# The latents' weights turned and split in six pieces over the query products, turned blocks tied behind the newest low part

## The chip, the cores and the metric

One core of one Trainium2 chip runs the whole program. The metric is device time in microseconds (us), the median of several executions. The engines in the text are TensorE (PE, matmuls), VectorE (DVE), ScalarE (ACT), GpSimd (POOL) and SyncE (SP, which here only issues DMAs).

## The reference, cut to what matters

The program is one decoder layer at 256 positions and width 2048, in float32: a mixer of two attention branches, a cross-attention over 256 memory tokens, and a SwiGLU feed-forward part, each followed by a layer norm.

```python
proj = x @ w_in                                    # 2048 -> 9552 columns
q_dsa, c_kv, q_idx, k_idx, w_idx, q_m, k_m, v_m, ga, gb = jnp.split(proj, points, axis=-1)
...
q_lat = jnp.einsum('shd,hdc->shc', q, w_uk)        # w_uk: 8 heads x 128 x 256 latents
...
o = jnp.einsum('shc,hcd->shd', o_lat, w_uv)        # w_uv: 8 heads x 256 x 128
...
merged = g_a * (o_a @ w_o_dsa) + g_b * (o_b @ w_o_moba)
return merged @ w_out                              # 2048 x 2048
...
k, v = jnp.split(mem @ w_kv, 2, axis=-1)           # the memory tokens' keys and values
```

## The kernel before, in words

**Products.** Every product streams its weight matrix from HBM once, in chunks of 512 KB (`chunk_in`, `wide`). A chunk lands in a tile `raw` (5 buffers). It is then split into a high and a low part in a tile `hl` (4 buffers): ACT writes the high part (line 116) and DVE writes the low part, the rest (line 117, a two-operand instruction over 128x1024 values). `chunk_mm` (lines 221 to 223) then issues three matmuls for each pair of operands: high by high, high by low, low by high. That makes 12 matmuls of 512 columns for a chunk, two row halves times two blocks of the contraction. The stationary operand is the turned input, held in four "quads" (tiles `b8`, printed as `b`), each with a high and a low half, too.

**Turned blocks.** An input is needed with its contraction along the partitions. `turned` (lines 172 to 184) does it without PE: four DMAs load a block in a permuted order into a tile `turn` (2 buffers), four DVE transposes (line 181) write a tile `tr`, ACT writes the high half (line 182) and DVE the low half (line 184). The generator pauses at each `yield`. Three blocks of `x` are turned so in the first 35 us (`load_x`), four blocks of the memory tokens in the output projection `w_out` (`load_mem`, lines 785 to 795), and the results of many products on the way to the next one.

**The latents' weights.** `latent_weights` (lines 292 to 317) loads `w_uk` and `w_uv` (1 MB each) and works in four pieces: two with four transposes (line 309) and a split, two with a split alone. It is a generator in the queue `side`, which `product` steps once for each chunk. It waits four steps, so all four pieces fall in the eight chunks of the product for the compressed keys, whose end also holds the norm of those keys (lines 386 to 419): small instructions that go back and forth between DVE, ACT, POOL and PE. The pieces are read by `latent_heads`, the next generator in `side`.

**What sets the order.** Each engine executes its instructions in one fixed order. That order is no copy of the code's: a scheduler lays the instructions out by its own simulated times when the program is built, and it may put an instruction ahead of others that the code names first. `tc.issue_after(ins)` forbids that for a block: what is traced in it stands behind `ins` on its engine. Before, it is used only for two loads (lines 693 and 788). All DMAs in this text are issued from SP, also in one order.

Of the kernel before, what the change touches and what calls it, by code (L numbers as in the profile page):

```python
# [1 line left out]

# [1 line left out]

# [8 lines left out]
AF = mybir.ActivationFunctionType  # L13
ALU = mybir.AluOpType
# [3 lines left out]
S = 256  # L18
# [47 lines left out]
def trunk(ctx: ExitStack, tc: tile.TileContext, a, out: bass.AP):  # L66
    nc = tc.nc
# [6 lines left out]
    dram = ctx.enter_context(tc.tile_pool(name="dram", bufs=6, space=bass.MemoryType.DRAM))  # L74
    side = Side()
    last = [None]
    later = []

    def flush():
# [7 lines left out]
    def nm(s):  # L87
        count[0] += 1
        return f"{s}_{count[0]}"
# [13 lines left out]
    def f(ap):  # L103
        return ap.bitcast(F32)
# [9 lines left out]

    def split(hi, lo, src, eng=None):
        nc.scalar.activation(hi, src, AF.Copy)  # L116
        (eng or nc.vector).tensor_tensor(lo, src, f(hi), op=ALU.subtract)  # L117


    ident = const.tile([P, P], F32, name="ident")  # L120
# [6 lines left out]
    for tt in range(NT):  # L127
        k = P * (tt + 1)
# [43 lines left out]
    def turned(hi, lo, src, mixed):  # L172
        n = src.shape[0]
        t = work.tile([P, S // 32, P], F32, tag="turn", name=nm("turn"), bufs=NTURN)[:, :n // 32]
        for i in range(4):
            nc.sync.dma_start(t[32 * i:32 * i + 32], src[:, i * P:(i + 1) * P].rearrange("(t i) c -> i t c", i=32))  # L176
        yield
        tr = work.tile([P, 4, S], F32, tag="tr", name=nm("tr"))[:, :, :n]
        v = t.rearrange("p t (j k) -> p k t j", k=4) if mixed else t.rearrange("p t (k j) -> p k t j", k=4)
        for i in range(4):  # L180
            nc.vector.transpose(tr[:, i, :], v[:, i])  # L181
        nc.scalar.activation(hi, tr, AF.Copy)  # L182
        yield
        nc.vector.tensor_tensor(lo, tr, f(hi), op=ALU.subtract)  # L184
# [8 lines left out]
    def chunk_in(pieces, c, n, held=False, mixed=False, fine=None, eng=None):  # L193
        raw = stream.tile([P, KC, W], F32, tag="raw", name=nm("raw"), bufs=5)
        at = 0
        for w in pieces:
            m = w.shape[1]
            if mixed:
                g = c * KC // 4
                rows = w[g * W:(g + 1) * W, :].rearrange("(p k) n -> p k n", k=4)[:, c * KC % 4:c * KC % 4 + KC, :]  # L200
            else:
                rows = w[c * KC * P:(c + 1) * KC * P, :].rearrange("(k p) n -> p k n", p=P)
            for k in ([slice(i, i + 1) for i in range(KC)] if fine else [slice(0, KC)]):
                last[0] = nc.sync.dma_start(raw[:, k, at:at + m], rows[:, k, :])
                if fine:
                    next(fine, None)
            at += m
        t = b8() if held else stream.tile([P, D], F32R, tag="hl", name=nm("hl"), bufs=4)
        hi, lo = [t[:, i * KC * W:(i + 1) * KC * W].rearrange("p (k n) -> p k n", k=KC) for i in range(2)]
        for k in ([slice(i, i + 1) for i in range(KC)] if fine else [slice(0, KC)]):  # L210
            split(hi[:, k, :n], lo[:, k, :n], raw[:, k, :n], eng)
        return hi, lo

    def chunk_mm(o, act, tt, c, kts, n, w):
# [77 lines left out]
    def latent_weights():  # L292
        raw = b8(F32)
        rows = a["w_uk"][0].rearrange("h d c -> (h d) c")
        for i in range(4):
            nc.sync.dma_start(raw[32 * i:32 * i + 32].rearrange("p (t c) -> p t c", c=LAT // 4),
                              rows[:, i * LAT // 4:(i + 1) * LAT // 4].rearrange("(t i) c -> i t c", i=32))
        rawv = b8(F32)
        for cc in range(2):
            nc.sync.dma_start(rawv[:, cc * 1024:(cc + 1) * 1024].rearrange("p (h d) -> p h d", h=NH),  # L300
                              a["w_uv"][0].rearrange("h (c k) d -> k c h d", k=2)[cc])
        for _ in range(4):
            yield
        for cc in range(2):
            q = b8()
            tr = work.tile([P, 4, S], F32, tag="tr", name=nm("tr")).rearrange("p k t -> p (k t)")
            v = raw.rearrange("p (t j k) -> p k t j", k=2, j=32)[:, cc]
            for g in range(4):
                nc.vector.transpose(tr[:, g * S:(g + 1) * S], v[:, g * 8:(g + 1) * 8])
            split(q[:, :1024], q[:, 1024:], tr)  # L310
            ukT.append(q)
            yield
        for cc in range(2):
            q = b8()
            split(q[:, :1024], q[:, 1024:], rawv[:, cc * 1024:(cc + 1) * 1024])
            uv.append(q)
            yield

# [2 lines left out]
    def wide(wsrc, load, tail=2):  # L321
# [10 lines left out]
        for c in range(ND):  # L332
            raw = stream.tile([P, 2 * W], F32, tag="raw", name=nm("raw"), bufs=5)
            t = stream.tile([P, D], F32R, tag="hl", name=nm("hl"), bufs=4)
            hi, lo = t[:, :2 * W], t[:, 2 * W:]
# [7 lines left out]
                last[0] = nc.sync.dma_start(raw[:, cs], rows)  # L343
                load(c, i)
            for cs in parts:
                split(hi[:, cs], lo[:, cs], raw[:, cs])
            if c < ND - tail:
                for g in range(2):
                    mm(g, c, hi, lo)
# [306 lines left out]
    for j in range(4):  # L656
        cs = slice(j * W, (j + 1) * W)
# [5 lines left out]
    for j in range(4):  # L663
        cs = slice(j * W, (j + 1) * W)
# [3 lines left out]
        for tt in range(NT):  # L668
            g = stage()
# [6 lines left out]
        q = Quad()  # L676
        d = spill()
        for tt in range(NT):
            g = gb[tt]
# [120 lines left out]
    for j in range(4):  # L800
        cs = slice(j * W, (j + 1) * W)
# [55 lines left out]
    for j in range(DFF // W):  # L857
# [13 lines left out]
        q = Quad()  # L871
# [40 lines left out]
```

## Time and profile before

| | us |
|---|---|
| median of 3 runs | 1505.7 (1501.36 to 1506.67) |
| the profiled execution, its own time | 1505.91 |
| its span, first to last instruction | 1504.1 |
| PE busy | 1464.7 (97%) |
| DVE busy | 929.5 (62%) |
| ACT busy | 685.3 (46%) |

The span is what the profile sees. The time of the same execution is 1.8 us longer. Matmuls overlap in the pipeline, so PE's busy time is not a measure of how well PE is used; the number of matmuls in a stretch is.

### The profile page before, as it was taken

Reading aid. Unit: us, or ns where it says so; the run is one execution under the profiler, and the core shown is the slowest. Engines: PE = TensorE matmul, PEld = TensorE weight load, DVE = VectorE, ACT = ScalarE, POOL = GpSimd, SP = SyncE. Lnnn points to the kernel's source line nnn. Section 1 sums busy time; section 2 is a strip of 40 time slices with the busy share of each in tenths; the row PEclk is TensorE's granted clock in tenths of the full one; section 3 lists DMA queues with packets and bytes.
Section 4 is the critical chain, followed back from the end, with each engine's and each line's share of the span. In section 5 each row is a group of like instructions: output and inputs, shape, how many; then the busy total and the mean of one; then the engine's idle time right before and its main releaser. Section 6 shows DMA issues by size and latency. Waiting matters only on the chain.

```text
span 1504.1 us, 17772 instructions
## 1 busy us (share of the span) xinstructions
PE 1464.7 (97%) x6640; PEld 1216.3 (81%) x6640; DVE 929.5 (62%) x1145; ACT 685.3 (46%) x798; POOL 54.1 (4%) x63
## 2 busy tenths in 40 slices
PE   8999999999999999889989999999999999999996
PEld 6978888888888888677878888888888888888885
DVE  6565986575756665777784555555455455545455
ACT  4545456454544443354753444444344444333342
POOL 0000000000000000040020000000000000000003
PEclk9999999999999999999999999999999999999998
DMA  9875667777667789749536666666767667666662
GB/s 281 199 222 161 191 215 224 231 238 226 220 189 226 224 258 280 197 151 319 196 111 208 209 210 220 220 221 210 223 210 214 222 220 251 192 198 193 192 223 82
DMA packets 199703, 318.71 MB, mean 212 GB/s; under 512 B 18880, under 2 KB 60992, under 8 KB 199616
## 3 DMA queue, kind: packets, MB, share of 16 engines
q1 hardware_dynamic: 199616, 317.57, 68.4%
q8 instruction: 52, 0.85, 0.2%
q14 instruction: 35, 0.29, 0.1%
HBM read 299.70 MB, written 17.83 MB: 211 GB/s over the span
## 4 chain that ended last, share of the span: by engine, by line
PE 50%; DVE 3%; DMA 2%; issue 1%; ACT 0%; SPq 0%; POOL 0%; ACTq 0%; DVEq 0%
PE acc L222 16%; PE acc L223 16%; PE acc L221 16%; DVE b L735 1%; DMA spill<-b 1%; DVE b L778 1%; DMA spill<-stage 0%; DMA turn<-spill 0%; ACT b L116 0%; PE aux L156 0%; DVE b L117 0%; DVE hl L117 0%; DVE b L737 0%; SPq L176 0%; DVE b L780 0%
## 5 line engine op out<-in xcount | busy, mean ns | idle before, releaser
L117 DVE TENSOR_TENSOR hl<-raw,hl 128x1024 fp32r<-128x1024 f32 (+2 forms) x493 | 595.9, 1217 | 415.0 <-ACT hl L116 414.2
L116 ACT ACTIVATE hl<-raw 128x1024 fp32r<-128x1024 f32 (+2 forms) x495 | 516.6, 1051 | 582.9 <-PE acc L223 523.5
L222 PE MATMUL acc<-hl,b 128*128 128x512 f32 (+1 forms) x1912 | 746.9, 391 | 13.5 <-DVE hl L117 13.5
L221 PE MATMUL acc<-hl,b 128*128 128x512 f32 (+1 forms) x1912 | 745.1, 391 | 0.7 <-ACT b L116 0.7
L223 PE MATMUL acc<-hl,b 128*128 128x512 f32 (+1 forms) x1912 | 745.1, 390 | 0.0
L222 PEld LDWEIGHTS acc<-hl,b 128*128 128x128 f32 x1912 | 361.4, 189 | 88.9 <-DVE hl L117 16.4
L221 PEld LDWEIGHTS acc<-hl,b 128*128 128x128 f32 x1912 | 361.2, 189 | 74.3 <-ACT b L116 0.9
L223 PEld LDWEIGHTS acc<-hl,b 128*128 128x128 f32 x1912 | 361.3, 189 | 73.9
L181 DVE STREAM_TRANSPOSE tr<-turn 128x256 f32<-128x256 f32 (+1 forms) x156 | 71.2, 515 | 106.7 <-DMA turn<-spill 87.7
L182 ACT ACTIVATE b<-tr 128x1024 fp32r<-128x1024 f32 (+1 forms) x39 | 39.5, 1016 | 123.1 <-DVE tr L181 119.7
L184 DVE TENSOR_TENSOR b<-tr,b 128x1024 fp32r<-128x1024 f32 (+1 forms) x39 | 45.3, 1167 | 3.6 <-ACT b L182 3.0
L116 ACT ACTIVATE b<-aux 128x512 fp32r<-128x512 f32 (+1 forms) x44 | 23.2, 537 | 30.0 <-PE aux L262 16.5
L117 DVE TENSOR_TENSOR b<-aux,b 128x512 fp32r<-128x512 f32 (+1 forms) x44 | 25.9, 609 | 8.6 <-ACT b L116 8.3
L117 POOL TENSOR_TENSOR hl<-raw,hl 128x1024 fp32r<-128x1024 f32 x2 | 4.9, 2456 | 718.9 <-ACT hl L116 718.9
L222 PE MATMUL acc<-b,b 128*128 128x512 f32 x72 | 28.0, 391 | 0.3 <-DVE b L117 0.3
L221 PE MATMUL acc<-b,b 128*128 128x512 f32 x72 | 27.9, 393 | 0.1
L223 PE MATMUL acc<-b,b 128*128 128x512 f32 x72 | 27.9, 390 | 0.0
L117 DVE TENSOR_TENSOR b<-raw,b 128x1024 fp32r<-128x1024 f32 x16 | 23.4, 1484 | 6.7 <-ACT b L116 6.5
L261 PE MATMUL acc<-hl,b 128*128 128x512 f32 x64 | 26.0, 406 | 1.5 <-DVE hl L117 1.5
L262 PE MATMUL acc<-hl,b 128*128 128x512 f32 x64 | 25.6, 404 | 0.0
L261 PE MATMUL aux<-b,b 128*128 128x256 f32 (+1 forms) x80 | 21.9, 282 | 0.0
L262 PE MATMUL aux<-b,b 128*128 128x256 f32 (+1 forms) x80 | 21.0, 279 | 0.0
(135 smaller groups left out, 629.5 us busy)
## 6 DMA issues: line engine op xcount, KB each, us to landing
raw<-in_w_ffn_in SPq DMA_DIRECT2D x176, 512.0 KB, 4.6
raw<-in_w_in SPq DMA_DIRECT2D x143, 512.0 KB, 4.3
raw<-in_w_ffn_out SPq DMA_DIRECT2D x88, 512.0 KB, 4.4
raw<-in_w_out SPq DMA_DIRECT2D x32, 512.0 KB, 5.7
spill<-stage SPq DMA_DIRECT2D x56, 256.0 KB, 4.1
turn<-spill SPq DMA_DIRECT2D x112, 128.0 KB, 3.4
raw<-in_w_o_dsa SPq DMA_DIRECT2D x16, 512.0 KB, 4.5
raw<-in_w_o_moba SPq DMA_DIRECT2D x16, 512.0 KB, 4.8
```

The costliest lines, as they stand in the source:

```text
L116: nc.scalar.activation(hi, src, AF.Copy)
L117: (eng or nc.vector).tensor_tensor(lo, src, f(hi), op=ALU.subtract)
L181: nc.vector.transpose(tr[:, i, :], v[:, i])
L182: nc.scalar.activation(hi, tr, AF.Copy)
L184: nc.vector.tensor_tensor(lo, tr, f(hi), op=ALU.subtract)
L221: nc.tensor.matmul(o[:, :n], xh, hi[:, kk, :n], start=k == 0, stop=False)
L222: nc.tensor.matmul(o[:, :n], xh, lo[:, kk, :n], start=False, stop=False)
L223: nc.tensor.matmul(o[:, :n], xl, hi[:, kk, :n], start=False, stop=k == kts - 1)
L261: nc.tensor.matmul(o, lh, rl, start=False, stop=False)
L262: nc.tensor.matmul(o, ll, rh, start=False, stop=stop)
L735: nc.vector.tensor_tensor(t, t, self.rows[0][:, cs], op=ALU.mult)
L778: nc.vector.tensor_tensor(t, t, self.rows[0][:, cs], op=ALU.mult)
```

## The change: places in the order, and when the latents' weights are split

Three edits. A list `lows` records the DVE instruction of each chunk's low part as it is traced. `behind()` puts a block behind the newest one. The transposes in `turned`, those of `latent_weights`, and the DVE parts of the latter's splits are put in such blocks. And `latent_weights` waits eight steps in place of four, and pauses once more between the high and the low part of each `w_uk` piece, so it makes six pieces, in the query product that follows. No instruction is added or removed.

```diff
+    lows = []
...
     def split(hi, lo, src, eng=None):
         nc.scalar.activation(hi, src, AF.Copy)
-        (eng or nc.vector).tensor_tensor(lo, src, f(hi), op=ALU.subtract)
+        return (eng or nc.vector).tensor_tensor(lo, src, f(hi), op=ALU.subtract)
+
+    def behind():
+
+        return tc.issue_after(lows[-1].ins) if lows else nullcontext()
...
-        for i in range(4):
-            nc.vector.transpose(tr[:, i, :], v[:, i])
+        with behind():
+            for i in range(4):
+                nc.vector.transpose(tr[:, i, :], v[:, i])
         nc.scalar.activation(hi, tr, AF.Copy)
...
-            split(hi[:, k, :n], lo[:, k, :n], raw[:, k, :n], eng)
+            ins = split(hi[:, k, :n], lo[:, k, :n], raw[:, k, :n], eng)
+            if eng is None:
+                lows.append(ins)
...
-        for _ in range(4):
+        for _ in range(8):
             yield
         for cc in range(2):
             q = b8()
...
-            for g in range(4):
-                nc.vector.transpose(tr[:, g * S:(g + 1) * S], v[:, g * 8:(g + 1) * 8])
-            split(q[:, :1024], q[:, 1024:], tr)
+            with behind():
+                for g in range(4):
+                    nc.vector.transpose(tr[:, g * S:(g + 1) * S], v[:, g * 8:(g + 1) * 8])
+            nc.scalar.activation(q[:, :1024], tr, AF.Copy)
+            yield
+            with behind():
+                nc.vector.tensor_tensor(q[:, 1024:], tr, f(q[:, :1024]), op=ALU.subtract)
             ukT.append(q)
             yield
         for cc in range(2):
             q = b8()
-            split(q[:, :1024], q[:, 1024:], rawv[:, cc * 1024:(cc + 1) * 1024])
+            with behind():
+                split(q[:, :1024], q[:, 1024:], rawv[:, cc * 1024:(cc + 1) * 1024])
             uv.append(q)
             yield
...
             for cs in parts:
-                split(hi[:, cs], lo[:, cs], raw[:, cs])
+                lows.append(split(hi[:, cs], lo[:, cs], raw[:, cs]))
```

Where the order of an engine changes at all, it does so in three stretches: the first 35 us, the stretch around the latents' weights, and the output projection. Elsewhere the same instructions stand in the same order.

**Output projection, DVE.** `hl` rows are low parts of chunks of `w_out`, in the order of the chunks; `tr<-turn` rows are the transposes of the memory tokens' first two blocks; `b_730` and `b_739` rows are those blocks' low halves. Before:

```order
L117 TENSOR_TENSOR hl_4838<-raw_4836,hl_4838 128x1024
L181 STREAM_TRANSPOSE tr_4934<-turn_4912 128x256 x4
L117 TENSOR_TENSOR hl_4855<-raw_4853,hl_4855 128x1024
L184 TENSOR_TENSOR b_730_4911<-tr_4934,b_730_4911 128x1024
L117 TENSOR_TENSOR hl_4873<-raw_4871,hl_4873 128x1024
L117 TENSOR_TENSOR hl_4896<-raw_4894,hl_4896 128x1024
L181 STREAM_TRANSPOSE tr_4998<-turn_4976 128x256 x4
L117 TENSOR_TENSOR hl_4919<-raw_4917,hl_4919 128x1024
```

The same engine and place in the changed kernel:

```order
L118 TENSOR_TENSOR hl_4838<-raw_4836,hl_4838 128x1024
L118 TENSOR_TENSOR hl_4855<-raw_4853,hl_4855 128x1024
L118 TENSOR_TENSOR hl_4873<-raw_4871,hl_4873 128x1024
L118 TENSOR_TENSOR hl_4896<-raw_4894,hl_4896 128x1024
L118 TENSOR_TENSOR hl_4919<-raw_4917,hl_4919 128x1024
L187 STREAM_TRANSPOSE tr_4934<-turn_4912 128x256 x4
L118 TENSOR_TENSOR hl_4942<-raw_4940,hl_4942 128x1024
L732 SCALAR_TENSOR_TENSOR b_689_4608<-b_689_4608,acc_4744 128x512
L190 TENSOR_TENSOR b_730_4911<-tr_4934,b_730_4911 128x1024
```

The first four transposes moved behind four more low parts. Those of the second, third and fourth block moved behind four more low parts each in the same way (the second's from ahead of `hl_4919` to behind `hl_4983`). SP's order is the same there.

**Latents' weights, DVE.** `hl_787` and `hl_756` are the second chunk of the first query product in either order, `hl_819` and `hl_774` the third; `tr<-b` are transposes of `w_uk`, `b<-tr` the low parts of its pieces, `b<-b` those of `w_uv`; `stage`, `st`, `mv` and `kn` rows belong to the norm. Before:

```order
L117 TENSOR_TENSOR hl_787<-raw_785,hl_787 128x1024
L309 STREAM_TRANSPOSE tr_607<-b_70_526 128x256 x4
L309 STREAM_TRANSPOSE tr_633<-b_70_526 128x256 x4
...
L117 TENSOR_TENSOR b_84_632<-tr_633,b_84_632 128x1024
L117 TENSOR_TENSOR b_88_658<-b_71_531,b_88_658 128x1024
L398 BN_AGGR mv_106_724<-st_105_723 128x2
L402 TENSOR_SCALAR kn_696<-acc_506,mv_96_690,rst_97_693 128x64
L117 TENSOR_TENSOR b_91_679<-b_71_531,b_91_679 128x1024
L117 TENSOR_TENSOR hl_819<-raw_817,hl_819 128x1024
```

The same place in the changed kernel:

```order
L118 TENSOR_TENSOR hl_756<-raw_754,hl_756 128x1024
L318 STREAM_TRANSPOSE tr_748<-b_70_526 128x256 x4
L407 SCALAR_TENSOR_TENSOR stage_501<-acc_506,rst_663,kvg 128x256
L410 BN_STATS st_89_667<-acc_506 128x6
L411 BN_AGGR mv_90_668<-st_89_667 128x2
L322 TENSOR_TENSOR b_110_747<-tr_748,b_110_747 128x1024
L415 TENSOR_SCALAR kn_674<-acc_506,mv_90_668,rst_91_671 128x64
L407 SCALAR_TENSOR_TENSOR stage_502<-acc_507,rst_697,kvg 128x256
L410 BN_STATS st_99_701<-acc_507 128x6
L416 TENSOR_TENSOR kn_674<-kn_674,kig 128x64
L118 TENSOR_TENSOR hl_774<-raw_772,hl_774 128x1024
```

Between the second and the third chunk's low part there stood eight transposes and four low parts of the weights (with the `b_80` row that is left out); now four transposes and one low part stand there, with more of the norm. The other four transposes and three low parts follow between the low parts of the next four chunks.

**First stage, DVE.** `hl` rows are chunks two to nine of the first weights, counted from nought (`hl_164`, `hl_181`, `hl_205`, ..., `hl_268` is the seventh, `hl_290` the eighth); `tr<-turn` are blocks of `x`. In the changed kernel:

```order
L118 TENSOR_TENSOR hl_164<-raw_163,hl_164 128x1024
L187 STREAM_TRANSPOSE tr_183<-turn_144 128x256 x4
L118 TENSOR_TENSOR hl_181<-raw_180,hl_181 128x1024
L118 TENSOR_TENSOR hl_205<-raw_204,hl_205 128x1024
L190 TENSOR_TENSOR b_2_97<-tr_183,b_2_97 128x1024
...
L118 TENSOR_TENSOR hl_268<-raw_267,hl_268 128x1024
L118 TENSOR_TENSOR hl_290<-raw_289,hl_290 128x1024
L187 STREAM_TRANSPOSE tr_309<-turn_270 128x256 x4
L118 TENSOR_TENSOR hl_307<-raw_306,hl_307 128x1024
```

Before, the transposes `tr_183` stood ahead of `hl_164` and `tr_309` ahead of `hl_268`. On SP the third block's four loads now stand behind the seventh chunk's load and ahead of the eighth's, where three of the four stood ahead of the seventh's, and one more 256 KB load of a bias stands ahead of the eighth's.

## Rows read from the trace of the kernel before

**Rows 1.** PE's waits, whole span: engine line <- releaser: us in total, times, longest.

```profile
PE acc L222 <- DVE hl L117: 13.5, 6, 3.8
...
PE acc L261 <- DVE hl L117: 1.5, 1, 1.5
```

**Rows 2.** Stretches: us, busy us (x instructions) by engine, granted clock, DMA share, GB/s.

```profile
560.00:580.00 20.00, 20.00 (x90) 16.57 (x89) 13.81 (x16) 8.56 (x9) 0.00 (x0) 1.00 0.96 333
580.00:600.00 20.00, 19.45 (x86) 15.77 (x85) 10.61 (x12) 7.09 (x7) 0.00 (x0) 1.00 0.82 227
600.00:620.00 20.00, 16.39 (x60) 12.70 (x59) 13.98 (x19) 6.55 (x7) 0.00 (x0) 0.83 0.66 169
620.00:640.00 20.00, 18.38 (x81) 14.91 (x80) 15.72 (x18) 8.77 (x10) 0.00 (x0) 1.00 0.80 230
...
81.82:87.60 5.78, 5.78 (x14) 4.54 (x15) 4.63 (x12) 1.68 (x3) 0.00 (x0) 0.50 0.76 226
```

**Rows 3.** Timeline of PE, output projection: start us, us, [idle before <-releaser].

```profile
595.34 0.50 PE L222 MATMUL acc<-hl,b 128*128 128x512 f32 x1 [0.55 <-DVE hl L117]
...
607.42 0.79 PE L222 MATMUL acc<-hl,b 128*128 128x512 f32 x1 [3.62 <-DVE hl L117]
...
628.59 0.50 PE L222 MATMUL acc<-hl,b 128*128 128x512 f32 x1 [1.62 <-DVE hl L117]
```

**Rows 4.** Timeline of DVE, output projection.

```profile
592.01 2.17 DVE L181 STREAM_TRANSPOSE tr<-turn 128x256 f32<-128x256 f32 x4 [5.97 <-DMA turn<-in_mem]
594.10 1.18 DVE L117 TENSOR_TENSOR hl<-raw,hl 128x1024 fp32r<-128x1024 f32 x1
```

**Rows 5.** Timeline of ACT, output projection.

```profile
586.44 1.06 ACT L116 ACTIVATE hl<-raw 128x1024 fp32r<-128x1024 f32 x1 [1.66 <-PE acc L223]
```

**Rows 6.** DMA issues, 575 to 600 us: xcount, KB each, median us to landing.

```profile
raw<-in_w_out SPq DMA_DIRECT2D x8, 512.0 KB, 7.9
turn<-in_mem SPq DMA_DIRECT2D x8, 128.0 KB, 7.4
```

**Rows 7.** Timeline of PE, first query product.

```profile
78.21 0.73 PE L221 MATMUL acc<-hl,b 128*128 128x512 f32 x2
81.82 0.80 PE L222 MATMUL acc<-hl,b 128*128 128x512 f32 x1 [2.88 <-DVE hl L117]
```

**Rows 8.** Timeline of DVE, first query product.

```profile
71.49 2.72 DVE L309 STREAM_TRANSPOSE tr<-b 128x256 f32<-128x256 f32 x8
...
74.64 1.20 DVE L117 TENSOR_TENSOR b<-tr,b 128x1024 fp32r<-128x1024 f32 x1
...
80.55 1.22 DVE L117 TENSOR_TENSOR hl<-raw,hl 128x1024 fp32r<-128x1024 f32 x1
```

**Rows 9.** Timeline of ACT, first query product.

```profile
72.94 1.06 ACT L116 ACTIVATE b<-tr 128x1024 fp32r<-128x1024 f32 x1 [0.46 <-DVE tr L309]
...
77.11 1.04 ACT L116 ACTIVATE hl<-raw 128x1024 fp32r<-128x1024 f32 x1
78.48 1.06 ACT L116 ACTIVATE hl<-raw 128x1024 fp32r<-128x1024 f32 x1 [0.33 <-DMA raw<-in_w_in]
```

**Rows 10.** Timeline of POOL, norm of the keys.

```profile
72.84 0.56 POOL L150 TENSOR_TENSOR rst<-rst,mhalf 128x1 f32<-128x1 f32 x1
...
74.72 1.53 POOL L150 TENSOR_TENSOR rst<-rst,mhalf 128x1 f32<-128x1 f32 x1
```

**Rows 11.** Timeline of PE, first stage.

```profile
17.99 1.07 PE L260 MATMUL acc<-hl,b 128*128 128x512 f32 x4
```

**Rows 12.** Timeline of DVE, first stage.

```profile
14.63 1.23 DVE L117 TENSOR_TENSOR hl<-raw,hl 128x1024 fp32r<-128x1024 f32 x1
...
28.10 2.20 DVE L181 STREAM_TRANSPOSE tr<-turn 128x256 f32<-128x256 f32 x4 [2.16 <-DMA turn<-in_x]
```

**Rows 13.** Timeline of ACT, first stage.

```profile
27.63 1.06 ACT L116 ACTIVATE hl<-raw 128x1024 fp32r<-128x1024 f32 x1 [3.15 <-DMA raw<-in_w_in]
```

**Rows 14.** Timeline of PE, behind the first layer norm.

```profile
673.62 0.50 PE L222 MATMUL acc<-hl,b 128*128 128x512 f32 x1 [3.77 <-DVE hl L117]
```

More of the change, by code (lines that the diff above doesn't have):

```diff
@@ L1 @@
-from contextlib import ExitStack
+from contextlib import ExitStack, nullcontext
 import numpy as np
```

## The prediction

> **What bounds the kernel now.** I read the waits of PE first, because PE is busy nearly all the time and what it does not do is little enough to be listed. The reader sees that nearly all that stops it in a product is one thing: DVE has not written the low part of a chunk. Line 222 waited so six times, 13.5 us in all, and line 261 once, 1.5 us [rows 1]. So PE is the bound, and a gain can come only from these few waits and from what the clock does behind them.
>
> The second view is that of stretches. From 560 to 580 us PE issues 90 matmuls, 20/90 = 0.222 us each. The next three stretches of 20 us hold 86, 60 and 81 [rows 2]. That is 43 fewer than three times 90, or 43 x 0.222 = 9.55 us lost in the output projection. The granted clock shows why this is more than the waits: it is 1.00 at 560 to 580 us (2.4 GHz) and 0.83 on the mean from 600 to 620 us [rows 2], and the waits there are 0.55, 3.62 and 1.62 us, 5.8 us together [rows 3]. The rest is matmuls at half the clock behind the longest of them.
>
> The third view is the timeline of each waiting place. In the output projection DVE stood idle for 5.97 us until a DMA of the memory tokens had landed, did four transposes in 2.17 us, and wrote the next low part only at 594.10 us [rows 4]. The high part of that chunk had begun at 586.44 us [rows 5]. The low part was not late for its own data; it stood behind transposes whose data had not come. In the first query product the low part of the third chunk began at 80.55 us [rows 8], behind eight transposes and four low parts of the latents' weights, while its high part had begun at 77.11 us [rows 9]; PE idled 2.88 us for it [rows 7]. Then 14 matmuls took 5.78 us at clock 0.50, that is 1.2 GHz [rows 2]: 14 x 0.222 = 3.11 us at full clock, so 2.67 us more. The two together are 5.55 us.
>
> **The change, part by part.**
>
> *Output projection, transposes four chunks later.* I take a chunk's time as 12 x 0.222 = 2.67 us. Had nothing stood ahead of it, the low part would have ended at 586.44 + 1.06 + 1.23 = 588.7 us. It ended at 594.10 + 1.18 = 595.3 us, and PE had idled only 0.55 us by 595.34 [rows 3, 4]. So PE has 594.8 - 588.7 = 6.1 us in hand on each low part. In the new order the first transposes stand behind the low part of three chunks on, which ends near 588.7 + 3 x 2.67 = 596.7 us; their data landed by 592.0 us [rows 4]. They wait for nothing, and end near 598.9 us. The next high part is ready at 586.44 + 4 x 2.67 + 1.06 = 598.2 us, so its low part is 0.7 us late against 6.1 in hand. More falls on DVE in one place when a product ends: two sums and two statistics, for which I put 2.5 us (an estimate, four instructions at half the 1.23 us of a low part), beside 2.17 of transposes and 1.2 of a low half, 5.9 us together, and DVE gains 2.67 - 1.23 = 1.44 us on every chunk in between. It stays inside the 6.1.
>
> *The loads there.* SP's order is the same, but it is now in time: chunk loads wait for a low part five chunks back, so they go out near 588.7 us, land 7.9 us later [rows 6] near 596.6, and are read at 586.44 + 5 x 2.67 = 599.8 us. The next four loads of memory tokens follow them and land 7.4 us after issue [rows 6], near 599 us; their transposes stand behind the seventh low part, near 604.7 us. A `turn` tile is held longer, by four chunks, and SP would stop at its third use until 598.9 us; the chunk load behind it is due at 588.7 + 4 x 2.67 = 599.4 us. So nothing is held. Value: all 9.55 us. Bounds: 3 us if only the first and the last wait (0.55 + 1.62, and some of the clock) go, and 9.55.
>
> *Latents' weights, pieces spread over the chunks.* Four of the eight transposes (2.72/2 = 1.36 us) and three of four low parts (3 x 1.2 = 3.6 us) leave the place ahead of the third chunk [rows 8]. What stays ahead of it is a chain with the norm: transposes to 72.9, the high part of the piece 72.94 to 74.0 [rows 9], its low part to 75.5, then an instruction of the norm that waits for POOL, then another. POOL's power took 0.56 us alone and 1.53 us when it began 0.08 us after a low part on DVE [rows 10]. I take 1.53 for the first (a low part runs beside it) and 0.56 for the second: 74.6 + 1.53 = 76.1, 0.3 for the normed value, 0.2 + 0.56 for the second power, 0.9 for three small instructions: the third low part can start near 78.0 us. Its high part is the other condition: begun at 77.11 at the latest [rows 9], it ends by 78.15. From 78.2 us the low part ends at 79.4; PE ran dry at 81.82 - 2.88 = 78.94 us [rows 7]. So 0.5 us of idle stays. The fourth chunk's high part ends at 79.54 [rows 9], and its low part follows four transposes (1.36 us) and two small instructions, from 80.9 to 82.1 us against about 82.1 on PE: I add 0.2 for it and the next ones. A wait of 1.62 us left the clock at 1.00 in its stretch [rows 2, 3], so 0.5 brings no fall. Value: 5.55 - 0.7 = 4.85 us. Bounds: 0 (the wait and the fall come back) and 5.55. The pieces that come later cost nothing as long as PE does not reach the products that read them, which stand about 25 us on.
>
> The Trainium skill's page "SBUF — State Buffer", section "SBUF: two separate sides", speaks against this part: DVE with two SBUF inputs and GpSimd share one port pair under an exclusive lock, and whichever starts second is blocked for the whole instruction. The trace agrees (0.56 against 1.53 us), since the new order puts a low part right ahead of an instruction that waits for POOL. Without the lock the chain would end 1 us earlier, near 77.0 us, and the high part alone would decide, so the sum is the same within 0.5 us.
>
> *First stage.* Here the old order cost 1.5 us, the wait of line 261 [rows 1]: transposes at 28.10 us waited 2.16 us for the third block, and the seventh chunk, whose high part began at 27.63, stood behind them [rows 12, 13]. That goes. But transposes now follow the low part of the second chunk, 14.63 + 1.23 = 15.9, and end at 18.0 us; the third chunk's ends at 19.2 us, where PE wants it at 17.99 + 4 x 0.222 = 18.9 [rows 11, 12]: 0.3 us new. The eighth chunk's load has one more load of 256 KB ahead of it on SP, half a chunk's bytes, so it comes perhaps 0.5 to 1.5 us later, and the third block's transposes (2.20 us) stand ahead of the ninth low part: I put 1.2 us for both. Value: 0. Bounds: 1.5 us gained and 1.5 us lost.
>
> *Sum.* 9.55 + 4.85 + 0 = 14.4 us off the profiled execution's own 1505.91 us (1504.1 of span and 1.8 around it): 1491.5 us. That execution lay 0.2 us over the median of the runs, so the forecast is **1491 us**, 0.97% faster. The low parts of all other turned blocks keep their places, so the rest of the 1504 us has no reason to move.
>
> **The rivals.**
>
> *The wait at the latents' weights stays.* In the new order DVE waits for POOL twice ahead of the third low part. If these waits are 2 us longer than worked out, PE idles as before and the clock falls. Against it: only POOL's slow power is near, at 0.97 us. Time: 1505.7 - 9.55 + 0 = 1496 us.
>
> *The output projection gives back half.* DVE's load at a product's end meets the transposes and uses up the 6.1 us, and a fall of the clock follows: half of 9.55 stays, 1505.7 - 4.8 - 4.85 = 1496 us. For it speaks the 5.9 us above, against it the 1.44 us that each chunk gives.
>
> *The change does not do what it says.* The transposes are not late in the new order, but the chunks' loads themselves bind in these stretches, or PE waits elsewhere for what came late. Then 1503 to 1507 us. Against it: DVE's idle names the block's DMA, not the chunk's [rows 4].
>
> *Slower: SP stops.* A `turn` tile is freed four chunks later, and SP has one order. If block loads hold SP past the 6.1 us in hand and the 3 us of early landing, chunk loads starve PE at every one of the four blocks, each 3.62 of wait and 2.67 of clock, 25 us in place of 9.55: 1505.7 + 15.6 - 4.85 = 1516 us. It decides when SP is held over 9 us beyond a chunk's due time; worked out above, it is held for none.
>
> **How the numbers follow.** Forecast 0.68, latents' wait stays 0.12, half given back 0.06, no change 0.10, slower 0.04. The likeliest case's own range is 1488 to 1494.5: first stage 1.5 either way, and one stretch at 1.2 GHz more or less (2.67 us), since waits like that of 3.77 us behind the layer norm [rows 14] move in time and the fall behind them may last otherwise. The range is 1486 to 1498 us: it takes in the first three cases. A measurement tells 0.5% (7.5 us) from no change; faster than 1498.2 us are the first three cases, 0.85 after a little for their edges; same 0.11; slower 0.04.
>
> **What would show it.** Right: no stretch of 20 us from 560 to 640 us (moved by some 5 us) under 88 matmuls; no DVE idle before transposes of the memory tokens; granted clock 1.00 throughout both places; line 222's waits down from 13.5 to about 5 us in all, the one of 3.77 left. Wrong in the latents' part: a wait over 2 us on line 222 near 79 us, with DVE idle for POOL. Wrong in the first stage: new waits on line 261 near 19 and 32 us that together pass 3 us.

## The result, and the profile after

The changed kernel takes 1490.97 us (median; 1489.91 to 1494.76 in 4 runs) beside 1506.18 us for the kernel before (1501.36 to 1507.73 in 4 runs). The ratio is 0.9909, with a 95% interval of 0.988 to 0.9937: 0.9% faster, against 0.97% forecast. The profiled execution took 1489.91 us, 16.0 us less than that of before.

These are PE's waits over the whole span, with the columns of [rows 1]. Line 222 of before is line 230 now, line 261 is line 269, line 117 is line 118.

```profile
PE acc L230 <- DVE hl L118: 5.8, 3, 3.8
...
PE acc L269 <- DVE hl L118: 0.4, 2, 0.2
```

Low parts of chunks stopped PE for 15.0 us before and for 6.2 us now. The wait of 3.8 us is that of [rows 14]. The next rows are the stretches, with the columns of [rows 2]; their engines are PE, its weight loads, DVE, ACT and POOL, in this order:

```profile
560.00:580.00 20.00, 20.00 (x89) 16.54 (x89) 14.90 (x17) 8.74 (x9) 0.00 (x0) 1.00 1.03 361
580.00:600.00 20.00, 20.00 (x90) 16.56 (x89) 14.90 (x19) 9.06 (x9) 0.00 (x0) 1.00 1.10 254
600.00:620.00 20.00, 20.00 (x90) 16.57 (x89) 17.48 (x23) 10.28 (x10) 0.00 (x0) 1.00 0.84 233
620.00:640.00 20.00, 20.00 (x90) 16.57 (x89) 14.00 (x17) 8.06 (x8) 0.00 (x0) 1.00 0.67 209
640.00:660.00 20.00, 15.83 (x71) 12.40 (x70) 18.44 (x15) 11.96 (x17) 16.53 (x12) 0.89 0.29 84
```

The output projection, which held 86, 60 and 81 matmuls in three stretches, holds 90 in each, all at 2.4 GHz. From there on the first stretch that loses any is that of the layer norm behind it. DVE's timeline in the output projection shows why. No row there has an idle time ahead of transposes any more, where [rows 4] had 5.97 us:

```profile
588.78 1.23 DVE L118 TENSOR_TENSOR hl<-raw,hl 128x1024 fp32r<-128x1024 f32 x1 [1.50 <-ACT hl L117]
589.92 2.19 DVE L187 STREAM_TRANSPOSE tr<-turn 128x256 f32<-128x256 f32 x4
592.03 1.19 DVE L118 TENSOR_TENSOR hl<-raw,hl 128x1024 fp32r<-128x1024 f32 x1
```

In the first query product PE's timeline lists no wait from 60 to 130 us. DVE reaches the third chunk's low part at 76.01 us (80.55 before, [rows 8]). Of these 4.5 us, 1.7 were gained earlier: the second chunk's low part began at 68.68 us in place of 70.35. From there to the third it is 7.33 us now and was 10.20. DVE waits on the way three times for POOL:

```profile
71.77 0.48 DVE L407 SCALAR_TENSOR_TENSOR stage<-acc,rst,kvg 128x256 f32<-128x256 f32 x1 [0.53 <-POOL rst L155]
...
72.53 1.19 DVE L322 TENSOR_TENSOR b<-tr,b 128x1024 fp32r<-128x1024 f32 x1
74.44 0.34 DVE L415 TENSOR_SCALAR kn<-acc,mv,rst 128x64 f32<-128x64 f32 x1 [0.72 <-POOL rst L155]
75.35 0.48 DVE L407 SCALAR_TENSOR_TENSOR stage<-acc,rst,kvg 128x256 f32<-128x256 f32 x1 [0.56 <-POOL rst L155]
...
76.01 1.22 DVE L118 TENSOR_TENSOR hl<-raw,hl 128x1024 fp32r<-128x1024 f32 x1
```

The experiments below use one more sum. For each matmul I took the time from its start to the next one's start, less the median of that for matmuls of its width (0.227 us for 512 columns), and added these excesses up by stretch. It is PE's lost time, waits and lower clock together, in us. Each row is a single execution, the profiled one. A wait counts here from start to start, so it comes out some 0.2 us longer than the idle time in PE's timeline:

| profiled execution | first stage, 8 to 45 us | latents, 45 to 130 | output projection, 560 to 640 | norm behind it, 640 to 705 | 705 to 800 |
|---|---|---|---|---|---|
| before | 3.8 | 5.4 | 9.5 | 6.7 | 11.5 |
| after | 2.2 | 0.3 | -0.1 | 10.4 | 8.3 |
| ties on the turned blocks only | 2.1 | 4.1 | 0.0 | 11.2 | 8.5 |
| latents' weights only | 2.1 | -0.1 | 9.7 | 10.6 | 8.3 |
| ties on the memory blocks only | 4.3 | 2.7 | -0.1 | 9.1 | 8.3 |
| six pieces, their ties left out | 2.2 | 4.4 | -0.1 | 10.2 | 10.2 |
| ties, four steps | 6.3 | 4.5 | -0.1 | 12.6 | 10.6 |
| two chunks back | 4.5 | 0.4 | -0.1 | 9.7 | 8.3 |
| memory blocks in place | 4.0 | 4.3 | 3.9 | 9.8 | 10.0 |
| transposes twice | 2.5 | -0.1 | 3.2 | 11.4 | 8.3 |
| norm's additions shared | 4.5 | -0.2 | -0.1 | 4.5 | 10.2 |
| after, again | 5.5 | 0.3 | -0.1 | 11.6 | 8.3 |
| norm's additions shared, again | 2.4 | -0.1 | -0.1 | 5.1 | 8.2 |

The columns are fixed times. Behind the output projection the changed kernel runs some 16 us ahead of the kernel before, so the same work can fall into another column there.

### The profile page after: what moved, and what is told of

It reads as the page before. It is cut to its first block, busy times and chain, and to the rows that moved or that the text cites. A ratio compares the mean times of both kernels' runs of the same rounds, so it can differ in the third digit from the quotient of the medians.

```text
span 1488.1 us, 17774 instructions
## 1 busy us (share of the span) xinstructions
PE 1456.6 (98%) x6640; PEld 1209.5 (81%) x6640; DVE 927.8 (62%) x1145; ACT 685.4 (46%) x798; POOL 52.5 (4%) x63
## 4 chain that ended last, share of the span: by engine, by line
PE 50%; DVE 3%; DMA 2%; issue 1%; SPq 0%; ACT 0%; POOL 0%; DVEq 0%
PE acc L230 17%; PE acc L231 17%; PE acc L229 17%; DMA turn<-spill 1%; DVE b L748 1%; DVE b L791 1%; DVE b L118 1%; DMA spill<-stage 1%; DMA spill<-b 0%; DVE b L750 0%; DVE hl L118 0%; SPq L181 0%; DVE lnst L733 0%; DVE b L732 0%; DVE b L793 0%
## 5 line engine op out<-in xcount | busy, mean ns | idle before, releaser
L269 PE MATMUL aux<-b,b 128*128 128x256 f32 (+1 forms) x80 | 21.8, 281 | 0.0
L875 ACT ACTIVATE stage<-acc 128x512 f32<-128x512 f32 x22 | 13.2, 599 | 18.1 <-PE acc L231 18.1
```

Source lines behind the costliest of these rows:

```text
L269: nc.tensor.matmul(o, lh, rl, start=False, stop=False)
```

## The experiments

**The two halves apart.** The first kernel has of the change only the ties of the turned blocks; `latent_weights` is as before:

```diff
-        for i in range(4):
-            nc.vector.transpose(tr[:, i, :], v[:, i])
+        with behind():
+            for i in range(4):
+                nc.vector.transpose(tr[:, i, :], v[:, i])
```

The second has all edits of `latent_weights`, and `turned` is as before:

```diff
-        for _ in range(4):
+        for _ in range(8):
...
+            with behind():
+                for g in range(4):
+                    nc.vector.transpose(tr[:, g * S:(g + 1) * S], v[:, g * 8:(g + 1) * 8])
+            nc.scalar.activation(q[:, :1024], tr, AF.Copy)
+            yield
+            with behind():
+                nc.vector.tensor_tensor(q[:, 1024:], tr, f(q[:, :1024]), op=ALU.subtract)
...
```

> Only the transposes of turned blocks are tied; the latents' weights are split as before. Theory (DVE's order decides, each place by itself): the output projection keeps 89 or 90 matmuls in each 20 us, so its 9.55 us are gone, the first stage is within 2 us of before, and the wait of 2.9 us with matmuls at 1.2 GHz behind it stays in the first query product: 1495 to 1497 us. Rival (the gain comes from spreading the latents' pieces, and the tied transposes only move the waits): 1500 us or more, with stretches under 85 matmuls left in the output projection.

> Only the latents' weights are changed (eight steps, six pieces, tied); the transposes of turned blocks are not tied. Theory: line 222's wait near 79 us and the half clock behind it go, 5.0 to 5.5 us, and the output projection loses its 9.5 us as before: 1500 to 1502 us. Rival (a wait for POOL takes the place of the weights): a wait over 2 us near 79 us and 1504 us or more.

Measured: 1496.49 us (9 runs), ratio 0.9915 [0.9884, 0.9945], for the ties on the turned blocks; 1502.64 us (10 runs), ratio 0.9963 [0.9938, 0.9987], for the latents' weights. PE's timeline of the first kernel has the old wait of [rows 7] and none in the output projection:

```profile
79.89 0.80 PE L230 MATMUL acc<-hl,b 128*128 128x512 f32 x1 [2.88 <-DVE hl L118]
```

The second has the reverse. These are its stretches in the output projection:

```profile
580.00:600.00 20.00, 16.69 (x73) 13.38 (x72) 11.30 (x15) 6.26 (x7) 0.00 (x0) 0.98 0.68 169
600.00:620.00 20.00, 17.61 (x71) 13.85 (x70) 15.04 (x20) 6.91 (x8) 0.00 (x0) 0.93 0.81 208
620.00:640.00 20.00, 20.00 (x83) 16.40 (x83) 13.91 (x14) 8.80 (x9) 0.00 (x0) 0.92 0.77 230
```

It holds 43 matmuls fewer than three times 90, as before, though the waits fall elsewhere. So each half removes its own loss and nothing of the other's. The medians are 11.9 and 5.7 us under that of the kernel before beside them, 17.6 us together; the whole change, timed later on the same chip (`after, again`), is 16.3 us under it.

**The memory blocks alone.** Of the turned blocks only those of the memory tokens are tied, and `latent_weights` is as before.

```diff
+        with behind() if pin else nullcontext():
+            for i in range(4):
+                nc.vector.transpose(tr[:, i, :], v[:, i])
...
-                g = turn(q, mem[:, j * W:(j + 1) * W])
+                g = turn(q, mem[:, j * W:(j + 1) * W], pin=True)
```

> Of the turned blocks only the four of the memory tokens are tied; everything else is as before. Theory: the output projection's 9.55 us are gone as with all blocks tied, PE's losses before 100 us are those of before: about 1496.5 us in one run. The difference to the run with all turned blocks tied is what the first stage is worth, 0 by the prediction, within 1.5 us either way. Rival (the other turned blocks matter): 2 us or more of the gain missing after 100 us.

Measured: 1495.27 us in one run, no loss in the output projection, the wait of 2.87 us near 79 us there. The gain in the output projection is that of the memory blocks; the ties on `x` and on the other turned blocks are not needed for it.

**Eight steps without ties, ties without eight steps.** From the changed kernel, one of the two parts of the latents' edit is taken back each time. First the ties of the pieces are left out:

```diff
-            with behind():
-                for g in range(4):
-                    nc.vector.transpose(tr[:, g * S:(g + 1) * S], v[:, g * 8:(g + 1) * 8])
+            for g in range(4):
+                nc.vector.transpose(tr[:, g * S:(g + 1) * S], v[:, g * 8:(g + 1) * 8])
...
-            with behind():
+            if True:
                 nc.vector.tensor_tensor(q[:, 1024:], tr, f(q[:, :1024]), op=ALU.subtract)
...
-            with behind():
+            if True:
                 split(q[:, :1024], q[:, 1024:], rawv[:, cc * 1024:(cc + 1) * 1024])
```

In another kernel the eight steps are four again:

```diff
-        for _ in range(8):
+        for _ in range(4):
```

> All of the change but the ties in the latents' weights: eight steps and six pieces, untied. In the built order all eight transposes and four low parts then stand ahead of the third chunk's low part again. Theory (the place in DVE's order decides): a wait of about 2.9 us near 79 us and 14 matmuls at 1.2 GHz come back, about 1496 us. Rival (that the generator pauses later and in more pieces is what helps): no wait there, 1491 us.

> The whole change, but the latents' weights wait four steps as before and not eight; their ties stay. In the built order all eight transposes and four low parts then stand ahead of the third chunk's low part again, since the tie names a low part from an earlier product. Theory (the place in DVE's order decides): a wait of 2.5 to 3 us near 79 us comes back, with or without matmuls at 1.2 GHz behind it, 1494 to 1497 us. Rival (the ties alone do it): no wait there, 1491 us.

Measured: 1496.08 and 1503.33 us, one run each. PE's wait is back in either; the two rows are from the first and the second kernel:

```profile
79.95 0.80 PE L230 MATMUL acc<-hl,b 128*128 128x512 f32 x1 [2.88 <-DVE hl L118]
```

```profile
84.79 0.74 PE L230 MATMUL acc<-hl,b 128*128 128x512 f32 x1 [2.88 <-DVE hl L118]
```

DVE's timelines of the first and the second show all eight transposes together again, ahead of the third low part. In the second the ties are there and hold nothing back: the transposes are traced in the product for the compressed keys, so the newest low part that their tie can name is one of that earlier product.

```profile
69.62 2.73 DVE L317 STREAM_TRANSPOSE tr<-b 128x256 f32<-128x256 f32 x8
```

```profile
74.46 2.73 DVE L318 STREAM_TRANSPOSE tr<-b 128x256 f32<-128x256 f32 x8
```

So the latents' gain needs both. The second kernel's 1503.33 us lies 6 us over the range expected, and the wait does not explain that: its first stage lost 6.3 us and the two columns behind the output projection 23.2 us (2.2 and 18.7 in the changed kernel). With one run the cause stays open.

**Half the distance.** The memory blocks' ties name the third newest low part, so the transposes stand two chunks later than before, not four.

```diff
-    def behind():
-        return tc.issue_after(lows[-1].ins) if lows else nullcontext()
+    def behind(back=1):
+        return tc.issue_after(lows[-back].ins) if lows else nullcontext()
...
-                g = turn(q, mem[:, j * W:(j + 1) * W])
+                g = turn(q, mem[:, j * W:(j + 1) * W], back=3)
```

> The whole change, but the memory tokens' transposes are tied to the low part two chunks older, so they stand behind two more chunks than before the change and not four. Theory (each low part has 6.1 us in hand, and the block's loads land 5 us ahead of the changed place): the transposes wait up to 1 us for their loads and PE waits for nothing there, 89 or 90 matmuls in each 20 us, 1490 to 1492 us. Rival (only the full distance helps): stretches under 88 matmuls and 1493 us or more.

Measured: 1491.84 us in one run, 90 matmuls in each stretch from 560 to 640 us. DVE does wait for the memory tokens, at each of the four blocks (1.12, 1.32, 0.66 and 2.02 us), longer than the 1 us expected:

```profile
588.33 2.17 DVE L187 STREAM_TRANSPOSE tr<-turn 128x256 f32<-128x256 f32 x4 [1.12 <-DMA turn<-in_mem]
...
596.74 1.14 DVE L187 STREAM_TRANSPOSE tr<-turn 128x256 f32<-128x256 f32 x2 [1.32 <-DMA turn<-in_mem]
...
615.27 2.17 DVE L187 STREAM_TRANSPOSE tr<-turn 128x256 f32<-128x256 f32 x4 [2.02 <-DMA turn<-in_mem]
```

It costs nothing: what counts is that DVE's idle time stays inside PE's lead over it, not that there is none.

**The transposes without their DMA.** From the kernel before: the memory blocks' transposes read a tile that was loaded once, earlier, so they have no load of their own to wait for. What it leaves out: keys and values are built from that one block four times over.

```diff
+    memt = const.tile([P, S // 32, P], F32, name="memt")
+    for i in range(4):
+        nc.sync.dma_start(memt[32 * i:32 * i + 32], mem[:, i * P:(i + 1) * P].rearrange("(t i) c -> i t c", i=32))
...
+        if held is not None:
+            t = held
...
-                g = turn(q, mem[:, j * W:(j + 1) * W])
+                g = turn(q, mem[:, j * W:(j + 1) * W], held=memt)
```

> The kernel before, with no ties, but the transposes of all four memory blocks read one block that was loaded long before (so keys and values are built from that block four times over); the four blocks' loads are still issued. The transposes then stand as early in DVE's order as before or earlier. Theory (what cost 9.55 us is DVE standing behind transposes that wait for a DMA, not the transposes' own time or place): no DVE idle there, PE keeps 88 to 90 matmuls in each 20 us of the output projection, about 1496.5 us, with the wait near 79 us as before. Rival (the place costs by itself, since four transposes ahead of a low part make it late): waits of line 222 between 570 and 640 us, 1500 us or more.

Measured: 1501.41 us in one run, with 3.9 us lost in the output projection: neither none nor all of the 9.5. The theory had expected none. The scheduler now put the transposes earlier and close together, as DVE's timeline shows, and PE waited twice behind them:

```profile
565.77 2.16 DVE L183 STREAM_TRANSPOSE tr<-turn 128x256 f32<-128x256 f32 x4 [2.55 <-DMA turn<-spill]
567.86 2.18 DVE L183 STREAM_TRANSPOSE tr<-memt 128x256 f32<-128x256 f32 x4
...
579.93 4.23 DVE L183 STREAM_TRANSPOSE tr<-memt 128x256 f32<-128x256 f32 x8
584.10 1.17 DVE L117 TENSOR_TENSOR hl<-raw,hl 128x1024 fp32r<-128x1024 f32 x1
```

```profile
585.33 0.50 PE L224 MATMUL acc<-hl,b 128*128 128x512 f32 x1 [2.19 <-DVE hl L117]
592.25 0.50 PE L224 MATMUL acc<-hl,b 128*128 128x512 f32 x1 [1.19 <-DVE hl L117]
```

All 16 transposes of the memory blocks run from 567.86 to 584.2 us; before, the four groups began at 592, 604, 615 and 625 us. They stand behind a wait of 2.55 us for another block that the kernel before has too. So the order is not that of before, and this is no clean subtraction of the wait. What it shows is that without any wait for the memory tokens' DMA 3.9 us are lost, against 9.5 with it: that much can come from DVE work that stands close together. How the 9.5 us divide between the wait for the DMA and the transposes' own time, these runs do not show.

**How much DVE work fits.** In the changed kernel each memory block is turned twice over.

```diff
-            for i in range(4):
+            for i in list(range(4)) * (2 if twice else 1):
                 nc.vector.transpose(tr[:, i, :], v[:, i])
```

> The changed kernel with each of the four memory blocks turned twice over: eight transposes in place of four into the same tile, so DVE has 2.17 us more to do for each block (8.7 us in all) in the output projection, and waits for nothing more. Theory (what was lost there was the wait of transposes for their DMA, and PE has 6.1 us in hand on each low part, so DVE's own work there is covered): no wait of PE over 0.3 us in the output projection, 88 or more matmuls in each 20 us of it, time as the changed kernel's, 1488 to 1495 us. Rival (the place was short of DVE time, and the change only just fits): waits of 1 us or more come back at two of the blocks or more, with 2 to 5 us lost there, 1493 to 1500 us.

Measured: 1494.19 us in one run. The rival is nearer: 3.2 us are lost in the output projection, from start to start, in three waits of PE.

```profile
616.39 0.50 PE L230 MATMUL acc<-hl,b 128*128 128x512 f32 x1 [0.85 <-DVE hl L118]
625.42 0.50 PE L230 MATMUL acc<-hl,b 128*128 128x512 f32 x1 [0.58 <-DVE hl L118]
629.20 0.50 PE L230 MATMUL acc<-hl,b 128*128 128x512 f32 x1 [0.77 <-DVE hl L118]
```

The first stands behind the third block's transposes, the other two behind the fourth's. From 600 to 620 us DVE was busy for 19.98 of 20 us (17.48 in the changed kernel):

```profile
600.00:620.00 20.00, 19.15 (x85) 15.54 (x84) 19.98 (x29) 8.57 (x10) 0.00 (x0) 1.00 0.80 212
```

So of 8.7 us more work some 5.5 fitted, by an estimate (8.7 less the 3.2 lost). The lead is not there anew for each low part: a block that uses it leaves less to the next, and it comes back only in time that DVE has left over.

**The norm behind the output projection.** In the changed kernel the largest wait of PE behind the first microseconds is that of [rows 14], where the norm's additions of a bias run on POOL. Every second one of the first norm's moves to DVE; it was timed twice, the second time beside the changed kernel.

```diff
-            eng = nc.vector if self.i > 0 and j % 2 else nc.gpsimd
+            eng = nc.vector if j % 2 else nc.gpsimd
             eng.tensor_tensor(t, t, self.rows[1][:, cs], op=ALU.add)
```

> The whole change, and besides half of the first layer norm's bias additions move from GpSimd to VectorE. The largest wait left is there: three low parts stand behind eight products of the norm that take 11.56 us, 1.45 us each, where one takes 0.69 us when GpSimd adds nothing. Theory (the place decides here too, and the products are slow because of the additions beside them): eight products and four additions take 9 to 10.5 us, PE's wait of 3.77 us falls to 2 to 3 us, 1487 to 1490 us. Rival (the additions are only moved, and DVE is busy as long): 1490 to 1493 us.

> The changed kernel once more, on the chip on which the next one is timed. Expected: 1490 to 1493 us, with 8 to 12 us of PE's time lost around the two norms behind the output projection, and none in it.

> The changed kernel with every second one of the first norm's bias additions on DVE in place of GpSimd, once more, beside the changed kernel on the same chip. Theory (GpSimd's additions are late for the turned blocks that DVE, and so PE, wait for behind the first norm): 2 to 5 us under the changed kernel, with 4 to 6 us lost around that norm in place of 9 to 12, and no change elsewhere. Rival (the earlier difference was a clock that happened to stay up in one run): within 1.5 us of the changed kernel.

Measured: 1487.97 us, ratio to before 0.9868 [0.9845, 0.9891]; then on one chip 1488.84 us, 0.9865 [0.9841, 0.9889], beside 1492.45 us, 0.9886 [0.9862, 0.9909], for the changed kernel. The medians are 3.0 and 3.6 us under the changed kernel's, and the intervals overlap; the first 3.0 are between different batches. Of the eight executions of this version five lie under all eight of the changed kernel.

PE's wait is shorter, 2.85 us in both profiles in place of 3.77; this one is from the second:

```profile
655.36 0.50 PE L230 MATMUL acc<-hl,b 128*128 128x512 f32 x1 [2.85 <-DVE hl L118]
```

The next rows are DVE and POOL in the changed kernel and then DVE in the shared one. They give busy time and mean ns of one, by line: the products from 642 to 662 us, the low parts of the changed kernel from 654.5 to 657 us, those of the shared one from 642 to 662 us. The row between is POOL's timeline of the changed kernel.

```profile
L748 DVE TENSOR_TENSOR b<-b,b 128x512 f32<-128x512 f32 x8 | 11.5, 1490 | 0.4 <-ACT b L747 0.4
L118 DVE TENSOR_TENSOR hl<-raw,hl 128x1024 fp32r<-128x1024 f32 x2 | 4.5, 2287 | 0.0
```

```profile
644.07 14.08 POOL L750 TENSOR_TENSOR b<-b,b 128x512 f32<-128x512 f32 x8 [1.44 <-issue]
```

```profile
L748 DVE TENSOR_TENSOR b<-b,b 128x512 f32<-128x512 f32 x8 | 9.5, 1221 | 0.4 <-ACT b L747 0.4
L118 DVE TENSOR_TENSOR hl<-raw,hl 128x1024 fp32r<-128x1024 f32 x4 | 4.8, 1211 | 0.0
```

The two low parts that ran beside POOL's last additions took 2.29 us each. In the shared kernel POOL's additions are over before the first low part, and each takes 1.21. The table's column behind the output projection shows more than this, 4.5 and 5.1 us lost in place of 10.4 and 11.6. But only about 1 us of that is the wait itself; the rest is waits further on and the clock, which differ from run to run. Besides, the second pair of profiles are the slowest of four runs of the changed kernel (1494.69 us) and the fastest of the shared one (1484.31). That this version is faster than the kernel before is clear; that it is some 3 us faster than the changed one is likely.

## Why the prediction was right, point by point

The median met the forecast of 1491 us to 0.03 us, and that is luck: the same program, timed again, took 1492.45 us, and terms that the forecast had at nothing moved and cancelled.

**Output projection, 9.55 us.** Right in size, and in the cause as far as the runs go: the place of the transposes. The stretches lost 9.5 us by the sum over matmuls and lose none now. (The 0.222 us is 20/90, where a stretch also counts a matmul that only reaches into it; from start to start it is 0.227 us, 0.2 us more in the sum.) The ties on the memory blocks alone bring all of it, the latents' edit none. Its reason needs two corrections. The transposes need not find their data landed; two chunks' distance, with up to 2.0 us of idle time on DVE, does as well. And the 6.1 us in hand is not there anew on each low part; the doubled transposes had used it up by the third block.

**Latents' weights, 4.85 us.** The mechanism was right, the term 0.3 us too small: 5.4 us were lost there and 0.3 are. The third low part came in time, but only just: the matmul that reads it began 0.3 us late, which is the loss in the table. I had left 0.5 us of idle for it and 0.2 for the next. DVE waited for POOL three times ahead of it, not twice; the first of these waits fell beside ACT's high part of the piece, which the chain needed anyway. POOL was slow once, as I put it, but in another instruction. Its powers took 0.55 us, and a one-operand instruction of 0.19 us took 1.07 when it began beside a low part on DVE.

```profile
70.91 0.19 POOL L154 TENSOR_SCALAR rst<-ssq 128x1 f32<-128x1 f32 x1 [68.51 <-ACT stage L404]
71.18 0.56 POOL L155 TENSOR_TENSOR rst<-rst,mhalf 128x1 f32<-128x1 f32 x1
72.70 1.07 POOL L154 TENSOR_SCALAR rst<-mv 128x1 f32<-128x1 f32 x1 [0.96 <-DVE mv L411]
73.85 0.55 POOL L155 TENSOR_TENSOR rst<-rst,mhalf 128x1 f32<-128x1 f32 x1
```

The delay of 0.88 us is the 0.97 of [rows 10] within a tenth, and the instruction ended at 73.77 us, 0.05 us behind the low part that ran from 72.53 to 73.72. The lock that the Trainium skill's page "SBUF — State Buffer" describes in "SBUF: two separate sides" fits both; the row corrects only which instruction the prediction put it on.

**First stage, 0.** The wait of line 269 fell from 1.5 us to 0.4 us. The new wait near 19 us that I put at 0.3 us is 0.17, and the eighth chunk's late load and the transposes behind it, for which I had put 1.2 us, cost one wait of 0.20:

```profile
18.10 0.50 PE L269 MATMUL acc<-hl,b 128*128 128x512 f32 x1 [0.17 <-DVE hl L118]
...
35.20 0.50 PE L269 MATMUL acc<-hl,b 128*128 128x512 f32 x1 [0.20 <-DVE hl L118]
```

The profiled execution gained 1.6 us there in all, outside my bound by a tenth. That is no gain of the order that the runs can tell: the same program, run again, lost 5.5 us there in place of 2.2, 1.39 us of it in a wait for the eighth chunk, whose DMA landed late, shown in PE's and in ACT's timeline of that run:

```profile
33.88 1.20 PE L268 MATMUL acc<-hl,b 128*128 128x512 f32 x4 [1.39 <-ACT hl L117]
```

```profile
32.77 1.06 ACT L117 ACTIVATE hl<-raw 128x1024 fp32r<-128x1024 f32 x1 [3.88 <-DMA raw<-in_w_in]
```

ACT waited 3.1 to 4.0 us for this chunk's DMA in all nine profiles with ties on `x`, and in four of them PE waited for it, too, for 0.4 to 1.4 us. So the late load is real, as forecast. In the four profiles without these ties PE waited 0.8 to 1.5 us for the seventh chunk's low part in its place. Over the table's rows the first stage lost 3.6 us on the mean with the ties and 3.6 without (2.1 to 6.3 and 2.1 to 4.3), so the value of 0 stands as far as these runs show.

**The rest, "no reason to move".** This was wrong: it moved, in two parts that nearly cancel. By the table's columns 3.7 us more are lost from 640 to 705 us and 3.2 less from 705 to 800. Some of that is only the columns' edge. Counted from the norm's first addition on POOL (660.60 us before, 644.07 after) it is 2.4 us more in 60 us and 1.8 less in the next 95. Of the 2.4, some 0.8 are clock: before, it was at 1.2 GHz for 3.4 us behind the wait of 3.77 us; now it fell 1.6 us ahead of that wait's end and stayed there for 6.8 us, 5.2 of them with matmuls. The rows are from before and after:

```profile
674.70:678.10 3.40, 3.40 (x10) 2.63 (x9) 3.40 (x4) 0.66 (x1) 0.00 (x1) 0.50 0.82 249
```

```profile
655.50:662.30 6.80, 5.23 (x12) 4.13 (x13) 6.80 (x6) 0.56 (x1) 2.65 (x2) 0.50 0.55 141
```

The other 1.6 are later waits. PE waited there once before, 1.03 us at 706.42 us, and waits twice now, 0.83 and 1.22 us. They are of the kind that this change removes elsewhere: transposes of a turned block stand ahead of a low part and wait for their DMA. The rows are DVE's and then PE's after:

```profile
689.66 1.42 DVE L187 STREAM_TRANSPOSE tr<-turn 128x256 f32<-128x256 f32 x4 [3.63 <-DMA turn<-spill]
```

```profile
692.25 0.50 PE L230 MATMUL acc<-hl,b 128*128 128x512 f32 x1 [1.22 <-DVE hl L118]
```

Before, the same transposes waited 3.44 us in the same place. The ties left them where they were, so here the change cures nothing. The 1.8 us less are further on, where the kernel before had two more stretches at 1.2 GHz (clock column 0.53 and 0.51), which the profile of the changed kernel does not have:

```profile
763.40:767.00 3.60, 3.60 (x16) 3.37 (x16) 3.60 (x8) 2.19 (x4) 0.00 (x0) 0.53 0.00 0
780.50:784.00 3.50, 3.50 (x13) 2.88 (x11) 2.77 (x5) 1.19 (x2) 0.00 (x0) 0.51 0.53 154
```

The forecast allowed for one stretch at 1.2 GHz more or less in its own range, but for none of these waits. The 16.0 us against 14.4 are the first stage's 1.6 and some 0.4 of the two main terms, less some 0.5 given back here.

**The rivals.** The latents' wait did not stay, the output projection gave nothing back, SP stopped nothing: no stretch from 560 to 640 us lacks a matmul.

## What to carry to other kernels

An engine that executes in one order passes an early-placed instruction's wait on to everything behind it. When PE waits for a low part, look at what stood ahead of it on DVE and what that waited for; the cure here was a place further back. Then compare the added work with the lead of the waiting engine, and with what DVE has left over, across the whole stretch: the lead is not there anew for each chunk. And an ordering constraint binds only against the instruction it names: where that one is long done by then, it is none, and a second edit has to move the code to the right product.

## What the runs showed of the hardware that was not expected

The price of one and the same wait differs from run to run. After 2.88 us without a matmul near 79 us, the kernel before ran 14 matmuls at 1.2 GHz [rows 2, 7]. The kernel with the turned ties alone ran 9 in 3.41 us (clock column 0.55), and the one with the memory ties alone none: 36 in 7.58 us, all at 2.4 GHz (clock column 1.00). These are the stretches behind the wait, in these two kernels:

```profile
79.89:83.30 3.41, 3.41 (x9) 2.73 (x10) 3.41 (x5) 0.97 (x2) 0.00 (x0) 0.55 0.73 189
```

```profile
82.42:90.00 7.58, 7.58 (x36) 6.29 (x36) 6.88 (x14) 3.00 (x4) 0.00 (x0) 1.00 0.84 240
```

By the table these three executions lost 5.4, 4.1 and 2.7 us there. So what follows the wait cost some 2.7, 1.4 and 0 us, and the wait between 2.7 and 5.4 us in all. Three more runs had the wait of 2.88 us (the six pieces without ties, the ties with four steps, the memory blocks in place) and lost 4.3 to 4.5 us. A forecast that counts on the clock's share needs that as its range; what decides it these runs don't tell.
